# HGRN scores: two of seven levels copied on ScalarE, and the fourth sums of pairs split one block later

## Chip, core and metric

The kernel runs on one core of a Trainium2 chip. The core has TensorE (PE) for matrix products, VectorE (DVE) and ScalarE (ACT) for elementwise work, GpSimd (POOL), and SyncE (SP), which starts most transfers. TensorE writes into PSUM, in banks that the other engines must empty; everything else lies in SBUF. The engines run side by side and wait for one another through semaphores; each takes its own instructions strictly in order. The metric is the device time of one execution in microseconds (us); smaller is better.

## What is computed

One inference step of a hybrid encoder layer: an mLSTM branch and an HGRN2 branch on 512 prompt frames and 32 sample frames, merged by gates. The change touches the HGRN branch. Its core, per head (8 heads, 128 channels each), with a running state `S` (key x value):

```python
def _hgrn_chunk(S, inp):
    q, k, v, lf = inp
    causal = jnp.tril(jnp.ones((L, L), dtype=bool))[:, :, None]
    g = jnp.cumsum(lf, axis=2)
    dec = jnp.exp(jnp.where(causal, g[:, :, :, None, :] - g[:, :, None, :, :], -jnp.inf))
    a = jnp.einsum('bhtc,bhtsc,bhsc->bhts', q, dec, k)
    o = jnp.einsum('bhtc,bhce->bhte', q * jnp.exp(g), S) + jnp.einsum('bhts,bhse->bhte', a, v)
    ...
```

`a` are the scores: each pair (query frame t, key frame s) is decayed per channel by the product of the forget gates between s and t. The inputs `q`, `k`, `v`, `lf` and the gates are columns of one large projection `xn @ w_in`, in fp32.

## The kernel before

**Projections.** The large projection is cut into units of 128 columns. An fp32 operand is split into a high part (a cast on ScalarE, L130) and a low part (a subtraction on VectorE, L131), and one product takes three matmuls. Most units are computed two at a time by class `Two` (L387), with seven products in place of eight: weights `a11`, `a12`, `a22` as they are and four sums `s1` to `s4` of weight tiles. In the trace the split sums are called `ws1..` to `ws4..`, the plain ones `wa11..`, `wa12..`, `wa22..`, each followed by the unit's number and `h` or `l`. A product is a block of 12 matmuls, in two halves of 6.

The class keeps the sums in five buffers (`NSUM`). `begin` (L397) loads `s1` and `s3` with a transfer by SyncE (L402) and an accumulating transfer by GpSimd (L403). `form` (L442) splits a weight; when `s2` has been split, `s4` is made in the same buffer by another accumulating transfer on GpSimd (L460) for pairs that are `early`; the last pair of all is `alone` and adds on VectorE (L462). `split_piece` (L125) takes its tiles from a ring of five (`NPIECE`).

**The order of blocks.** Class `Pump` (L551) merges the blocks of successive pairs. For the HGRN pairs the times in `PAIR` give, from one pair to the next, the order `s2, s1, s3, a11', a12', a22, s4` (a prime marks the next pair). `steps` (L596) calls `prepare` (L580) ahead of each block, which makes ready the weights of all blocks up to `AHEAD = 3` further on. So `s4` is prepared ahead of the matmuls of the next pair's `a11'`, and the block behind it, the next pair's `s2` with its `s1`, is prepared one block later. The casts and subtractions of a block are put under `issue_after(self.behind)` (L592): they may not be issued on ScalarE before the instruction `behind`.

**The chain of a head.** `chain(h)` (L1483) is a generator. What it yields is the number of half blocks that the pump runs before the chain goes on, so that its matmuls lie between those of the projections. It computes the scores by seven levels, `LEVELS = (1, 2, 4, 8, 16, 32, 64)`: at level c it copies every other run of c keys into `km` on ScalarE (L1500), multiplies them on TensorE with the queries of the neighbouring runs (L1511), and multiplies keys and queries by one more stretch of gates on VectorE (L1535). Of the product of 128 x 256, the entries whose row and column numbers have an exclusive or of at least c belong to this level or a later one; they are written into `at` by a masked copy on VectorE (L1542), the later levels over the earlier. At level 16 the mask is 32 columns wider, for the sample. `at` is set to zero on GpSimd at the start (L1487); at the end the triangles are cut out on GpSimd (L1479), which also zeroes the diagonal. Before each level's `km` the chain sets `pump.behind` to the `km` before it (L1498). After the levels come transposes of values and keys (L1587, copied to SBUF in L1590), the update of the state (`su`, L1606), the outputs (`ho`, L1630), their norm (`osb`, L1651), and the finish of the head before (`hoT`, L1659 and L1660), which lies behind level 16 of the next chain.

**What sets the order.** TensorE's order is written out by hand (`manual_schedule`). On the other engines a planner orders the instructions ahead of time: by priority and by the times at which its own model of the machine has them ready. The priority is the order in which the program is written, unless `high_priority` raises it, as it does for `km`, for the scores' copies and for the copies out of PSUM.

Of the kernel before, what the change touches and what calls it, by code (L numbers as in the profile page):

```python
# [17 lines left out]
P = 128  # L18
# [26 lines left out]
LEAD = 3  # L45
NPIECE = 5
AHEAD = 3
SCRATCH = 1024
RAWAHEAD = 4
WQ = 256  # L50
# [14 lines left out]
def hybrid_step(ctx: ExitStack, tc: tile.TileContext, a, o):  # L65
    nc = tc.nc
    V, S, G, PE = nc.vector, nc.scalar, nc.gpsimd, nc.tensor
# [10 lines left out]
    def slot(name, dt=F32):  # L78
        return sp.tile([P, SLOT], dt, tag="s", name=name)
# [5 lines left out]
    def small(name, shape, dt=F32, bufs=2, tag=None):  # L85
        return tp.tile(shape, dt, tag=tag or name, name=name, bufs=bufs)
# [11 lines left out]
    def paux(name):  # L98
        return pa.tile([P, 2, 512], F32, tag="a", name=name)
# [18 lines left out]
    def raw_piece(src, name):  # L118
        raw = wp.tile([P, WP], F32, tag="wr", name=name, bufs=NRAW)
        nc.sync.dma_start(raw[:, : src.shape[-1]], src)  # L120
        return raw
# [208 lines left out]
    class One:  # L330
# [22 lines left out]
        def prepare(self, i):  # L353
            def make(raw):
                if i == 0:
                    self.w = []
                self.w.append(split_piece(raw[self.unit, i], f"wi{self.unit}{i}"))

            return make
# [27 lines left out]
    class Two:  # L387
# [45 lines left out]
        def make(self, *forms):  # L433
            def go(raw):
                with tc.high_priority() if self.apart else nullcontext():
                    for form in forms:
                        if form not in self.w:
                            self.form(form, raw)

            return go  # L440

        def form(self, form, raw):  # L442
# [108 lines left out]
    class Pump:  # L551
# [28 lines left out]
        def prepare(self, upto):  # L580
            while self.made < min(upto, self.limit or len(self.order)):
                b = self.order[self.made]
                while self.begins and self.begins[0][0] <= self.made:
                    self.begins.pop(0)[1].begin()
                if b[1]:
                    need = self.loads.index(b[1][-1]) + 1
                    for u, i in self.loads[self.loaded : need + RAWAHEAD]:
                        self.raw[u, i] = raw_piece(w_in[u][:, i * WP : (i + 1) * WP], f"wi{u}r{i}")
                    self.loaded = max(self.loaded, min(need + RAWAHEAD, len(self.loads)))
                if b[2]:  # L590
                    after = self.pairs if isinstance(self.todo[self.ids[self.made][0]], Two) and self.pairs else self.behind
                    with tc.issue_after(after.ins) if after is not None else nullcontext():  # L592
                        b[2](self.raw)
                self.made += 1

        def steps(self):  # L596
            for i, b in enumerate(self.order):
                self.prepare(i + 1 + AHEAD)
                yield from b[3]()
# [15 lines left out]
        def run(self, chain):  # L615
            for n in chain:
                self.to(self.done + n)
# [554 lines left out]
    def level_masks():  # L1172
        lmask, smask = masks()
        sxt = small("sxt", [P, P + 2 * NS], bufs=1, tag="vsm")
        nc.sync.dma_start(sxt, a["sxt"])
        for i, c in enumerate(LEVELS):
            V.tensor_scalar(
                lmask[:, i, : 2 * P].rearrange("p (b t) -> p b t", b=2),
                sxt[:, :P].rearrange("p (o t) -> p o t", o=1).to_broadcast([P, 2, P]),
                float(c),  # L1180
                None,
                ALU.is_ge,
            )
        V.tensor_scalar(smask, sxt[:, P : P + NS], 0.5, None, ALU.is_ge)
        V.tensor_scalar(lmask[:, QUADS, 2 * P :], sxt[:, P + NS :], 0.5, None, ALU.is_ge)
        return lmask, smask

    with tc.manual_schedule(engines={mybir.EngineType.Activation, mybir.EngineType.DVE, mybir.EngineType.PE}):
# [15 lines left out]
        for k in range(KD):  # L1204
            t = xt[k]
# [129 lines left out]
    with tc.manual_schedule(engines={mybir.EngineType.PE}):  # L1335
        for h in range(MH):
# [35 lines left out]
            if h == 0:  # L1372
                with tc.issue_after(last.ins):
                    lmask, smask = level_masks()
# [6 lines left out]
    NA = NP // 2  # L1381
# [4 lines left out]
    def view(t, off, dims):  # L1386
        base = t[:, 0:T]
        return bass.AP(base.tensor, base.offset + off, [list(base.ap[0])] + [list(d) for d in dims])
# [94 lines left out]
    def chain(h):  # L1483

        tf, kk, q0, qq, kq, ii = (hs[h][k] for k in ("tf", "kk", "q0", "qq", "kq", "ii"))
        at = tp.tile([P, NA + P], F32, tag="bc", name=f"at{h}")
        G.memset(at, 0.0)  # L1487
        snap = small("snap", [P, 2, QUADS, NS], bufs=1, tag="ksm")
        dg = small("dg", [P, 5])
        told = tf[:, :T]  # L1490
# [3 lines left out]
        for li, c in enumerate(LEVELS):  # L1494
            smp = li == QUADS
            n = HB if smp else NA
            km = tp.tile([P, NA], F32, tag="vs", name=f"km{h}{c}", bufs=1)
            pump.behind = held[-1] if held else None  # L1498
            with tc.high_priority():
                low = S.copy(  # L1500
                    km.rearrange("p (n j c) -> p n j c", j=2, c=c),
                    view(kk, HB, ((2 * c, NA // (2 * c)), (c - HB, 2), (1, c))),
                )
                if li < QUADS:
                    S.copy(snap[:, :, li], hs[h]["pair"][:, :, csmp])
            held.append(low)
            yield STEPS[li]

            pn = paux(f"pl{h}{c}")
            for b in range(2):  # L1510
                PE.matmul(  # L1511
                    pn[:, 0, b * P : (b + 1) * P],
                    km[:, b * P : (b + 1) * P],
                    view(qq, b * P, ((2 * c, P // (2 * c)), (HB + c, 2), (1, c))),
                    start=True,
                    stop=True,
                )
            if smp:
                PE.matmul(pn[:, 0, NA:HB], kk[:, NA : NA + P], qq[:, csmp], start=True, stop=True)  # L1519
                ks, qs = (snap[:, i].rearrange("p l t -> p (l t)") for i in range(2))  # L1520
                PE.matmul(pn[:, 1, :P], ks, qs, start=True, stop=True)
            nb, na = (HB if c < NS else NA) // (2 * c), NA // (2 * c)
            tb, ta = told[:, : 2 * nb], told[:, told.shape[-1] - 2 * na :]
            tn = ttmp[:, base : base + nb + na]
            sides = ((tb, 0, nb, 1, 0), (ta, HB, na, 0, nb))
            with tc.high_priority():
                for t, lo, m, first, _ in sides:

                    x = view(
                        kk, lo + first * c, ((qoff + (1 - 2 * first) * c, 2), (2 * c, m), (1, c))  # L1530
                    )
                    d = bass.AP(
                        t.tensor, t.offset + 1 - first, [list(t.ap[0]), [2 * first - 1, 2], [2, m], [0, c]]
                    )
                    V.tensor_tensor(x, x, d, ALU.mult)  # L1535
                if told.shape[-1] == 2 * (nb + na):
                    t = told.rearrange("p (n t) -> p n t", t=2)
                    V.tensor_tensor(tn, t[:, :, 0], t[:, :, 1], ALU.mult)
                else:
                    for t, _, m, _, o_ in sides:  # L1540
                        V.tensor_tensor(tn[:, o_ : o_ + m], t[:, ::2], t[:, 1::2], ALU.mult)
                V.copy_predicated(at[:, :n], lmask[:, li, :n], pn[:, 0, :n])  # L1542
                if smp:
                    for i in range(QUADS):
                        d = slice(i * NS, (i + 1) * NS)
                        V.copy_predicated(at[d, NA:HB], smask[d], pn[d, 1, d])
            base += nb + na
            if c == NS // 2:
                tsmp = tn[:, nb - 1 : nb]
            told = tn  # L1550
            if li == 0:

                yield 1
                pn = paux(f"pd{h}")
                for b, c_ in enumerate([c_ for c_, _, _ in chunks] + [slice(NA, NA + P)]):
                    PE.transpose(pn[:, b // NB, b % NB * P : (b % NB + 1) * P], kq[:, c_], ident)
                with tc.high_priority():
                    V.tensor_reduce(
                        dg, pn.rearrange("p a t -> p (a t)")[:, : 5 * P].rearrange("p (b t) -> p b t", t=P), AX.X, ALU.add
                    )  # L1560
            if li == 4 and h:
                yield 1
                finish(h - 1)
# [40 lines left out]
        for b in range(NB):  # L1604
            c = slice(b * P, (b + 1) * P)
# [22 lines left out]
        for b, (c, i, j) in enumerate(chunks):  # L1628
            d = slice(b * P, (b + 1) * P)
# [56 lines left out]
    for k in range(2):  # L1686
        t = slot(f"p{k}")
# [17 lines left out]
    for f in range(KD):  # L1705
        w = weight(a["w_brh"][f], f"wbh{f}")
        acc = dense(w, 0, P, P, obs, f"yb{f}")
        t = gbs[f]
# [8 lines left out]
    for f in range(KD):  # L1717
        t = slot(f"h1{f}")
# [167 lines left out]
```

## Time and profile before

| quantity | us |
|---|---|
| median of three runs | 1139.38 (1138.98 to 1142.49) |
| the profiled execution | 1136.01 |
| its span, first to last instruction | 1134.3 |
| HGRN stage (640 to 955), of the span | 315 |
| of that: the last chain and the blocks behind it (864 to 955) | 91 |

The profile shows one execution. For each engine it gives the busy time, and for an instruction its start, its duration, and in brackets the time that its engine stood idle before it with what ended that time. A line such as `L1542 DVE COPY_PREDICATED at<-lmask,pl` names the line of the program, the engine, the operation, and the tiles written and read. A number behind the unit's name is left out in groups. The matmuls overlap: one of 272 columns is drawn with 0.29 us, though the next starts well before its end, so the distance between starts tells more than the durations.

### The profile page before, as it was taken

The page shows a single profiled execution, that of the slowest core. Times are in us where ns is not written, and L with a number is a line of the kernel's source. Part 1 is how long each engine was busy: PE and PEld are TensorE (multiplying, and loading weights), DVE is VectorE, ACT ScalarE, POOL GpSimd, SP SyncE. Part 2 cuts the span into 40 slices and gives each one's busy share as a digit, 9 for nine tenths or more (in the row PEclk, how much of TensorE's full clock was granted, in tenths as well). Part 3 has the DMA queues.
Part 4 walks back from the last instruction along what each step waited for, and adds up shares of the span by engine and source line. Part 5 has one row for each costly group of instructions (what it writes and reads, how often), then busy time and mean ns, then how long its engine had stood idle before and what let it go on. Part 6 is the DMA issues. An engine that isn't in the chain of part 4 may idle for free.

```text
span 1134.3 us, 24068 instructions
## 1 busy us (share of the span) xinstructions
PE 1116.8 (98%) x8849; PEld 1101.4 (97%) x8849; DVE 896.5 (79%) x2027; ACT 680.2 (60%) x1537; POOL 185.9 (16%) x363
## 2 busy tenths in 40 slices
PE   9999999999999999999999999999999999999998
PEld 8999999999999999999999999999998999999998
DVE  6887998576896786976888699999999867654585
ACT  5677557655666555665665477677766657333462
POOL 4842010100010100101000122223232220000000
PEclk9999999999999999999999999999999999999999
DMA  7134224323344142552767766666666686332743
GB/s 236 56 96 133 79 75 159 118 95 106 132 152 151 49 131 105 158 168 69 239 163 234 180 145 143 138 140 140 148 149 165 174 222 172 113 103 70 269 141 116
DMA packets 91006, 159.68 MB, mean 141 GB/s; under 512 B 10245, under 2 KB 17797, under 8 KB 90889
## 3 DMA queue, kind: packets, MB, share of 16 engines
q1 hardware_dynamic: 80928, 140.27, 38.3%
q0 software_dynamic: 9792, 17.83, 10.1%
q8 instruction: 69, 1.13, 0.4%
q14 instruction: 49, 0.39, 0.1%
q10 hardware_dynamic: 168, 0.06, 0.0%
HBM read 133.21 MB, written 24.91 MB: 139 GB/s over the span
## 4 chain that ended last, share of the span: by engine, by line
PE 78%; DVE 10%; DMA 5%; ACT 3%; issue 2%; POOL 0%; SPq 0%; ACTq 0%; DVEq 0%
PE d L485 29%; PE ya L151 8%; PE pg L1736 4%; PE q L151 4%; PE yb L151 4%; PE o L151 4%; PE C L902 4%; PE k L151 4%; DMA ws<-in_w_in 3%; PE sc L862 3%; PE nm L1077 2%; PE pl L1511 2%; PE d L370 1%; DVE cv L634 1%; PE ple L151 1%
## 5 line engine op out<-in xcount | busy, mean ns | idle before, releaser
L403 POOL DMA_DIRECT2D ws<-in_w_in x46 | 40.3, 876 | 230.3 <-DVE rsq_u L168 30.3
L499 ACT COPY t<-d 128x272 f32<-128x272 f32 x126 | 47.7, 379 | 3.2 <-PE d L485 3.1
L1535 DVE TENSOR_TENSOR hkq<-hkq,q 128x288 f32<-128x288 f32 (+1 forms) x96 | 40.8, 432 | 3.9 <-PE pl L1519 1.0
L634 DVE SCALAR_TENSOR_TENSOR cv<-ub,vec,cv 128x547 f32<-128x547 f32 x48 | 40.4, 842 | 1.3 <-ACT cv L629 0.6
L1511 PE MATMUL pl<-hkq,km 128*128 128x128 f32 x224 | 38.0, 292 | 1.8 <-ACT km L1500 1.7
L1511 PEld LDWEIGHTS pl<-hkq,km 128*128 128x128 f32 x224 | 31.1, 189 | 3.9 <-ACT km L1500 3.4
L1500 ACT COPY km<-hkq 128x256 f32<-128x256 f32 x56 | 24.0, 428 | 15.6 <-DVE hkq L1535 6.2
L1006 DVE SCALAR_TENSOR_TENSOR c<-c,wi,Cs 128x258 f32<-128x258 f32 x32 | 15.3, 479 | 20.0 <-PE Cs L1004 19.8
L460 POOL DMA_DIRECT2D ws<-in_w_in x22 | 23.2, 1055 | 41.0 <-DVE ws272l L131 27.4
L914 ACT COPY Co<-C 128x258 f32<-128x258 f32 x32 | 10.4, 378 | 29.1 <-PE C L902 22.3
L1145 DVE TENSOR_TENSOR y<-ya,y 128x272 f32<-128x272 f32 x48 | 19.1, 436 | 10.3 <-PE ya L151 9.2
L1542 DVE COPY_PREDICATED at<-lmask,pl 128x256 f32<-128x256 uint8 (+1 forms) x56 | 25.3, 451 | 0.0
L1088 ACT COPY y<-nm 128x516 f32<-128x516 f32 x16 | 9.5, 591 | 21.6 <-PE nm L1077 21.5
L799 POOL COPY vsm<-vt 128x96 f32<-128x96 f32 x16 | 6.0, 382 | 88.2 <-ACT vt L510 44.7
L1479 POOL TENSOR_SCALAR_AFFINE_SELECT aa<-at 128x128 f32<-128x128 f32 x32 | 18.8, 621 | 8.9 <-DVE at L1542 8.9
L1077 PE MATMUL nm<-vhl,sh 128*128 128x258 f32 x112 | 18.3, 285 | 0.0
L1036 DVE BATCH_NORM_STATS2 bs<-y 128x6 f32<-128x512 f32 (+1 forms) x20 | 13.8, 688 | 5.5 <-ACT y L1088 5.5
L1723 DVE TENSOR_TENSOR h<-o,h 128x272 f32<-128x272 f32 x16 | 6.3, 436 | 14.5 <-PE o L151 14.5
L978 POOL CAST vhl<-one 128x4 fp32r<-128x4 f32 x8 | 2.0, 244 | 95.8 <-PE nm L1077 95.8
L876 ACT CAST sh<-dm 128x512 fp32r<-128x512 f32 (+3 forms) x16 | 7.3, 459 | 16.6 <-DVE dm L870 16.6
L1641 ACT ACTIVATE osq<-kq 128x128 f32<-128x128 f32 x32 | 9.8, 305 | 12.3 <-DVE kq L1636 12.1
L1710 DVE TENSOR_TENSOR gb<-yb,gb 128x272 f32<-128x272 f32 x16 | 6.3, 436 | 13.1 <-PE yb L151 13.1
(4490 smaller groups left out, 5072.9 us busy)
## 6 DMA issues: line engine op xcount, KB each, us to landing
ws<-in_w_in POOLq DMA_DIRECT2D x68, 256.0 KB, 4.8
ws<-in_w_in SPq DMA_DIRECT2D x46, 256.0 KB, 3.6
ya_d<-y SPq DMA_DIRECT2D x32, 272.0 KB, 2.7
y<-ya_d SPq DMA_DIRECT2D x24, 272.0 KB, 3.7
c<-in_C SPq DMA_DIRECT2D x16, 258.0 KB, 3.9
out_Cp<-Co SPq DMA_DIRECT2D x16, 258.0 KB, 2.5
out_Cs<-c SPq DMA_DIRECT2D x16, 258.0 KB, 2.8
x<-in_xT SPq DMA_DIRECT2D x8, 272.5 KB, 4.7
```

Source lines behind the costliest of these rows:

```text
L151: PE.matmul(both[b][:m, :TH], part(w, off + k * step, m, x), xx[:, half(b)], start=(k == 0 and j == 0), stop=(k == n - 1 and j == 2),)
L403: G.dma_start(t, w_in[u][:, i * WP : (i + 1) * WP], accum_op=ALU.add)
L485: PE.matmul(ps, ww[:, c], xx, start=(start and k == 0 and j == 0), stop=end, skip_group_check=not start,)
L499: S.copy(t, ps)
L634: V.scalar_tensor_tensor(cv[:, :547], ub[:, j : j + 547], vcol(V_CW + 4 * ft + j), cv[:, :547], ALU.mult, ALU.add)
L862: PE.matmul(pn[:, 0, :n], ks[f][x][:, j * P : (j + 1) * P], qs[f][y][:, NS + j * P : T], start=(f == 0 and i == 0), stop=(f == KH - 1 and ...
L902: PE.matmul(pn[g][:, :VH], kw[b][x][:, f * P : (f + 1) * P], vv[b][y][:, g * VH : (g + 1) * VH], start=(b == 0 and j == 0), stop=(b == NB ...
L1077: PE.matmul(pn[:, g, :VH], st[j][x][:, (i - j) * P : (i - j + 1) * P], vv[j][y][:, g * VH : (g + 1) * VH], start=(j == 0 and q == 0), stop ...
L1511: PE.matmul(pn[:, 0, b * P : (b + 1) * P], km[:, b * P : (b + 1) * P], view(qq, b * P, ((2 * c, P // (2 * c)), (HB + c, 2), (1, c))), star ...
L1535: V.tensor_tensor(x, x, d, ALU.mult)
L1542: V.copy_predicated(at[:, :n], lmask[:, li, :n], pn[:, 0, :n])
L1736: PE.matmul(ps, part(w, k * P, P, x), xx[:, c], start=(k == 0 and j == 0), stop=(k == KD - 1 and j == 2))
```

## The change

Two edits, in the HGRN stage and in the blocks woven into it.

The scores: at the first level (c = 1), where the mask leaves out only the diagonal, the product is copied whole into the first 256 columns of `at` by ScalarE. At the last level (c = 64), where the mask is two off-diagonal blocks of 64 x 64 in each half, ScalarE copies these blocks, with one instruction for each half of the partitions. The five levels between keep the masked copy on VectorE. GpSimd sets only the last 128 columns of `at` to zero.

The fourth sums: for every `early` pair but the last, the block `s4` is prepared one block later, together with the block behind it; nothing behind it is prepared earlier or later than before.

```diff
+LATE = 2
...
+            go.late = self.early and not self.alone and forms == ("s4",)
             return go
...
         def prepare(self, upto):
             while self.made < min(upto, self.limit or len(self.order)):
                 b = self.order[self.made]
+                if getattr(b[2], "late", False) and self.made > upto - LATE:
+                    break
...
         at = tp.tile([P, NA + P], F32, tag="bc", name=f"at{h}")
-        G.memset(at, 0.0)
+        G.memset(at[:, NA:], 0.0)
...
-                V.copy_predicated(at[:, :n], lmask[:, li, :n], pn[:, 0, :n])
+                if li == 0:
+                    S.copy(at[:, :NA], pn[:, 0, :NA])
+                elif c == P // 2:
+                    for d, e in ((slice(0, c), slice(c, P)), (slice(c, P), slice(0, c))):
+                        S.copy(
+                            at[d, :NA].rearrange("p (b t) -> p b t", b=2)[:, :, e],
+                            pn[d, 0, :NA].rearrange("p (b t) -> p b t", b=2)[:, :, e],
+                        )
+                else:
+                    V.copy_predicated(at[:, :n], lmask[:, li, :n], pn[:, 0, :n])
```

## The prediction, made before the result

> **What bounds the kernel now.** I read the page's busy times first, then the busy times of the stretch in which the changed functions run, then the waits of TensorE in that stretch, and last, for each wait, the timeline of the engine that is named in it.
>
> ```profile
> span 1134.3 us, 24068 instructions
> PE 1116.8 (98%) x8849; PEld 1101.4 (97%) x8849; DVE 896.5 (79%) x2027; ACT 680.2 (60%) x1537; POOL 185.9 (16%) x363
> ...
> 640.00:955.00 315.00, 310.11 (x2488) 306.36 (x2487) 281.47 (x737) 214.84 (x568) 81.89 (x115) 1.00 0.67 156
> 640.00:864.00 224.00, 223.14 (x1796) 220.29 (x1795) 213.23 (x586) 159.68 (x441) 64.50 (x92) 1.00 0.64 144
> 864.00:955.00 91.00, 86.96 (x694) 86.07 (x693) 68.24 (x152) 55.17 (x129) 17.38 (x23) 1.00 0.73 183
> ```
>
> TensorE bounds it. The eight HGRN heads and the pairs of projections woven into them fill 640 to 955 us. The columns after the length are PE, PEld, DVE, ACT, POOL. PE idles 315 - 310.11 = 4.9 us there, 4.0 of them after 864. Counted by weight loads the slack is 315 - 306.36 = 8.6 us. The clock is 1.00 throughout, so nothing is to be had from it. VectorE is nearly full as well (213.23 of 224, 95%), ScalarE is at 71%. So the change can only win what is left of 4.9 to 8.6 us, and whatever it costs must stay under a bound of the same kind. [...]
>
> PE's idle is in few places. Rows of the timeline, the bracket being the idle time before the instruction and what ended it:
>
> ```profile
> 664.43 0.71 PE L1511 MATMUL pl<-hkq,km 128*128 128x128 f32 x4 [0.30 <-ACT km L1500]
> 726.95 0.71 PE L1511 MATMUL pl<-hkq,km 128*128 128x128 f32 x4 [0.40 <-ACT km L1500]
> 869.19 0.74 PE L1511 MATMUL pl<-hkq,km 128*128 128x128 f32 x4 [0.73 <-ACT km L1500]
> 872.46 0.75 PE L1511 MATMUL pl<-hkq,km 128*128 128x128 f32 x4 [0.25 <-ACT km L1500]
> 878.99 0.33 PE L1660 MATMUL hoT<-anti,osb 128*128 128x128 f32 x1 [1.44 <-DVE osb L1651]
> 921.30 0.39 PE L485 MATMUL d<-xfh,ws384h 128*128 128x272 f32 x1 [1.62 <-ACT t L499]
> ```
>
> They add up to 4.74 us: four waits for a key copy `km`, one for the normalised output `osb` of the last head but one, one for a copy of a pair's partial product.
>
> **Why km and osb are late.** The last chain, then an earlier head, ScalarE and VectorE in order of time:
>
> ```profile
> 866.31 0.79 DVE L1535 TENSOR_TENSOR hkq<-hkq,q 128x288 f32<-128x288 f32 x2
> 868.21 0.62 ACT L130 CAST ws480h<-ws 128x512 fp32r<-128x512 f32 x1 [2.80 <-DMA ws<-in_w_in]
> 868.73 0.40 ACT L1500 COPY km<-hkq 128x256 f32<-128x256 f32 x1
> 868.86 0.69 DVE L131 TENSOR_TENSOR ws480l<-ws,ws480h 128x512 fp32r<-128x512 f32 x1 [1.36 <-ACT ws480h L130]
> ...
> 725.63 0.42 DVE L1535 TENSOR_TENSOR hkq<-hkq,q 128x256 f32<-128x256 f32 x1
> 725.98 0.62 ACT L130 CAST ws475h<-ws 128x512 fp32r<-128x512 f32 x1 [1.79 <-DMA ws<-in_w_in]
> 726.50 0.40 ACT L1500 COPY km<-hkq 128x256 f32<-128x256 f32 x1
> ```
>
> `ws4..h` is the cast of a pair's fourth sum. Its data come by an accumulating DMA that is not there yet, so ScalarE stands for 2.80 us with `km` queued behind it, although `km`'s input was ready at 867.1; VectorE stands for 1.36 us in turn. At 726 it is the same in small: `km` could have gone at 726.05 and went at 726.50.
>
> **Part 1, the late split of the fourth sums** (`go.late`, `LATE`). It removes nothing and adds no instruction: per pair, one cast (ACT) and one subtraction (DVE) are prepared one block of 12 matmuls later, directly ahead of the next pair's first sums. What keeps the order on ScalarE is `issue_after(self.behind)`: the cast may not be issued ahead of the `km` copy that was last when the block was prepared. For the pairs of queries, and for the pair of 868, the move crosses the matmuls of level 2, so that the cast now comes behind that level's `km` instead of ahead of it. The consumers have room:
>
> ```profile
> 793.15 0.68 DVE L131 TENSOR_TENSOR ws477l<-ws,ws477h 128x512 fp32r<-128x512 f32 x1
> 798.39 0.29 PE L485 MATMUL d<-xh,ws477l 128*128 128x272 f32 x1
> ```
>
> 798.39 - 793.83 = 4.6 us against one block of about 2 us. In the last chain `km` then goes at 867.1, PE does not stand at 869.19, and VectorE is kept from 1.36 us of standing, but not wholly: ws480's data land at 868.2 in any case, and only small steps can fill the time before. From there to `osb` VectorE works without a gap, so what PE gets back at 878.99 is what VectorE gets back: bounds 0 (a fresh stall takes its place) and 0.73 + 0.25 + 1.44 = 2.42; I take **-1.2**, most of 1.36, as the rest is bound by the DMA. At 664 and 726 I take the visible waits, 0.30 + 0.40: **-0.7**, bounds 0 and -0.7. Each of these four waits also costs a slower restart (0.39 at 921.30 for a matmul that takes 0.29 in a run): 4 x 0.1 = **-0.4**, bounds 0 and -0.4.
>
> **Part 2, the scores.** Per head two of seven masked copies leave VectorE; ScalarE gets one copy of 128 x 256 and two of 64 partitions x 128. The memset of `at` shrinks from 384 to 128 columns on GpSimd, which is busy 82 of 315 us: nothing. Prices by rows of the same stretch:
>
> ```profile
> L1542 DVE COPY_PREDICATED at<-lmask,pl 128x256 f32<-128x256 uint8 (+1 forms) x56 | 25.3, 451 | 0.0
> ...
> L499 ACT COPY t<-d 128x272 f32<-128x272 f32 x66 | 25.1, 380 | 3.2 <-PE d L485 3.1
> L1500 ACT COPY km<-hkq 128x256 f32<-128x256 f32 x55 | 23.5, 427 | 15.6 <-DVE hkq L1535 6.2 <-DVE hr L169 4.0 <-DVE rsq_u L168 3.0
> L1594 ACT COPY kit<-ht 128x128 f32<-128x128 f32 x8 | 2.2, 272 | 0.0
> ...
> 729.22 0.45 DVE L1542 COPY_PREDICATED at<-lmask,pl 128x256 f32<-128x256 uint8 x1
> 729.55 0.29 DVE L1538 TENSOR_TENSOR q<-q 128x136 f32<-128x136 f32 x1
> 729.76 0.69 DVE L131 TENSOR_TENSOR wa1252l<-wi52r,wa1252h 128x512 fp32r<-128x512 f32 x1
> ...
> 730.25 0.29 PE L485 MATMUL d<-xl,wa1252h 128*128 128x272 f32 x1
> 730.50 0.39 PE L485 MATMUL d<-xh,wa1252l 128*128 128x272 f32 x1
> ...
> 853.56 0.29 PE L485 MATMUL d<-xl,wa1280h 128*128 128x272 f32 x1
> 853.83 0.40 PE L485 MATMUL d<-xh,wa1280l 128*128 128x272 f32 x1
> ...
> 921.30 33.46 PE d L485 x264
> ```
>
> A masked copy lasts 0.45 us, but the next instruction starts 0.33 after it, so VectorE is relieved by 0.66 us a head. The copy of the last level stands right ahead of `wa1252l`, which ends at 730.45, and PE's first matmul with it follows at 730.50: 0.25 after its neighbour, where the spacing in an unbroken run is 33.46 / 264 = 0.127 (the last row, from the chain of waits). So PE waits some 0.13 here and restarts 0.1 slower, in six heads alike, the last at 853.83: 6 x 0.23 = **-1.4**, bounds 0 and -1.4. On level 0 no wait of PE hangs on VectorE; nothing. ScalarE pays 0.38 (by `t`, also out of PSUM) + 2 x 0.27 (by `kit`, the same width out of PSUM, its lower end; 0.43 each by `km` is the upper) = 0.92 us a head. It has the room: 315 - 214.84 = 100 us idle over eight heads; and the copy of level 0 lies in a time when `km` waits for VectorE anyway. I take **0**, with the case in which the place is wrong as the first rival. The copies' own waits are for matmuls whose results VectorE waited for before; GpSimd's triangles now wait for ScalarE, at a time when it is ready earlier than VectorE was.
>
> **The tail.** In the blocks after the last chain a later fourth sum may hold SyncE, whose queue waits for that sum's buffer:
>
> ```profile
> 911.34 0.69 DVE L131 TENSOR_TENSOR ws490l<-ws,ws490h 128x512 fp32r<-128x512 f32 x1 [1.96 <-ACT ws490h L130]
> ...
> 912.06 0.33 SPq L402 DMA_DIRECT2D ws<-in_w_in  x1
> ...
> 912.91 0.42 SPq L1689 DMA_DIRECT2D p<-in_pT  x1
> ...
> 917.24 0.65 ACT L103 CAST ps0h<-p 128x544 fp32r<-128x544 f32 x1 [2.48 <-DMA p<-in_pT]
> ```
>
> The transfer of `p` follows the release at 912.03 within a microsecond, and the wait at 921.30 comes from ScalarE's 2.48 for it. If the release moves by a block (1.5 us without a chain), that wait grows by up to 1.5; if it comes earlier, it shrinks by up to 1.62. The cast already stands directly ahead of the next pair's first sum there, so I take **0**.
>
> **Sum:** -1.2 - 0.7 - 0.4 - 1.4 = -3.7 us. The profiled execution took 1136.01 (span 1134.3 and 1.7 around it), so it would take 1132.3. The median of the runs shown is 3.4 above it; the same step from 1139.38 gives **1135.7**.
>
> **Rivals.**
>
> *A. ScalarE becomes the pacer ahead of the state update.* Between the last `km` of a head and the copy of the transposed keys it runs without a gap:
>
> ```profile
> 787.13 0.62 ACT L130 CAST ws477h<-ws 128x512 fp32r<-128x512 f32 x1 [0.95 <-PE d L485]
> 788.14 0.41 ACT L1500 COPY km<-hkq 128x256 f32<-128x256 f32 x1 [0.39 <-DVE hkq L1535]
> ...
> 792.29 0.58 ACT L1590 COPY hkq<-ht 128x512 f32<-128x512 f32 x1
> ...
> 793.50 1.05 PE L1606 MATMUL su<-hi,hkq 128*128 128x128 f32 x8
> ```
>
> The copy ends at 792.87, 0.63 ahead of `su`. If the fourth sum's cast moves into this stretch (0.52, from 868.21 to 868.73) and the two copies come with 0.27 to 0.41 each (`kit`, and the `km` of 788.14), it is 1.06 to 1.34 late. PE then waits 0.43 to 0.71 in each of eight heads, and what was won ahead of `su` is spent there: +3.4 to +5.7, from 1139.38 some 1144. It decides from a delay of 0.63 on. For it: no gap and little slack; against it: the scalings of the values in that stretch are not urgent and the key copy has high priority, so that it may pass them.
>
> *B. The late split moves nothing.* ws475h went at 725.98 although the program prepares it ahead of a block that PE starts at 728: casts are placed when they are ready, not where they are written. Then only the scores act: -1.4 and a few tenths where 0.33 of VectorE helps `osb`: 1137.7, no change.
>
> *C. All waits go,* that of 921.30 too: -4.74 - 1.4 - 0.5 of restarts = -6.6, 1132.8. For it speaks that upstream relief moves the release at 912.03; against it that the order on ScalarE there is untouched.
>
> **How the numbers follow.** About 0.3% (3.4 us) is what a measurement of this kernel can tell from no change; the forecast lies just beyond. Forecast 0.45, of which 0.35 beyond the bound; A 0.25, slower; B 0.17, of which 0.15 no change; C 0.13, faster. Faster 0.50, same 0.25, slower 0.25. The range takes in C with the cap of 8.6 us (1130.8) and A to its upper price (1145.1): 1131 to 1145. The forecast's own range is 1134 to 1138, since its terms can each fall to nothing.
>
> **What would show it.** Right: no wait of PE on `km` at level 2 of the last chain, the cast of ws480 behind that `km`, the wait on `osb` down from 1.44 to a few tenths, `wa12..l` no longer ending as PE reaches it, DVE busy down by about 7 us and ACT up by about 7. Wrong: waits of `su` on the key copy (A), the casts ws4 in their old places (B), or waits of PE on first and second sums `ws1`, `ws2`, which now queue behind the fourth; also a reordering elsewhere in the planner's order that these steps don't see.

## The result, and the profile after

The changed kernel is slower: 1153.1 us median of four runs (1150.3 to 1153.46), against 1140.18 (1138.98 to 1142.49) for the kernel before, also four runs. The ratio is 1.0108, 95% interval [1.009, 1.0127]. The profiled execution took 1153.29 us. The page of the changed kernel, busy times first, then the busy times of the HGRN stretch (columns after the length: PE, PEld, DVE, ACT, POOL, clock):

```profile
span 1151.6 us, 24068 instructions
PE 1120.1 (97%) x8849; PEld 1103.0 (96%) x8849; DVE 894.8 (78%) x2011; ACT 686.0 (60%) x1561; POOL 180.0 (16%) x363
...
640.00:955.00 315.00, 295.07 (x2349) 289.53 (x2348) 266.69 (x698) 209.04 (x568) 75.25 (x114) 1.00 0.63 149
```

The span grew by 1151.6 - 1134.3 = 17.3 us. PE's idle time between 640 and 955 rose from 4.9 to 315 - 295.07 = 19.9 us, by weight loads from 8.6 to 25.5, which is 16.8 of the 17.3. So the loss lies in the changed stretch, and the clock, still 1.00, has no part in it. The window is the same 315 us, but the stage now ends later, so the window holds less of it: VectorE and ScalarE are less busy in it, not more. What PE waits for between 640 and 975, from the view of waits (us in all, times, longest):

```profile
PE pl L1515 <- ACT km L1504: 6.0, 9, 1.8
PE d L487 <- ACT t L501: 3.1, 2, 2.2
PE d L487 <- DVE ws288l L132: 1.9, 1, 1.9
PE ht L1601 <- POOL snap L1586: 1.3, 2, 0.7
PE d L487 <- DVE ws278l L132: 1.3, 1, 1.3
...
```

(The lines of the program have moved: 131 is now 132, 1500 is 1504, 1511 is 1515, 1535 is 1539, 1542 is 1555.) No wait on `osb` or on `wa12` is left, as predicted. New is a wait of about 1.25 us on the low half of a pair's second sum, in six heads alike (`ws274l` to `ws279l`) and of 1.9 on `ws288l`; new also are more waits on `km` and on the GpSimd copy `snap`. One of the six, in the changed kernel: first VectorE's timeline, then ScalarE's, then PE's.

```profile
782.10 0.69 DVE L132 TENSOR_TENSOR ws453l<-ws,ws453h 128x512 fp32r<-128x512 f32 x1
...
784.17 0.68 DVE L132 TENSOR_TENSOR ws177l<-ws,ws177h 128x512 fp32r<-128x512 f32 x1
784.77 0.68 DVE L1658 TENSOR_TENSOR kq<-kq,hr 128x512 f32<-128x512 f32 x1
...
786.95 0.68 DVE L450 TENSOR_TENSOR ws<-ws,wi77r 128x512 f32<-128x512 f32 x1
...
790.68 0.69 DVE L132 TENSOR_TENSOR ws277l<-ws,ws277h 128x512 fp32r<-128x512 f32 x1
...
781.00 0.41 ACT L1504 COPY km<-hkq 128x256 f32<-128x256 f32 x1 [2.05 <-DVE hkq L1539]
...
781.46 0.61 ACT L131 CAST ws453h<-ws 128x512 fp32r<-128x512 f32 x1
...
796.03 0.62 ACT L131 CAST ws477h<-ws 128x512 fp32r<-128x512 f32 x1 [2.15 <-DMA ws<-in_w_in]
...
791.43 0.39 PE L487 MATMUL d<-xfh,ws277l 128*128 128x272 f32 x1 [1.25 <-DVE ws277l L132]
```

The same places in the kernel before, VectorE, ScalarE, PE:

```profile
774.76 0.69 DVE L131 TENSOR_TENSOR ws453l<-ws,ws453h 128x512 fp32r<-128x512 f32 x1
...
775.68 0.69 DVE L131 TENSOR_TENSOR ws177l<-ws,ws177h 128x512 fp32r<-128x512 f32 x1
...
777.75 0.69 DVE L448 TENSOR_TENSOR ws<-ws,wi77r 128x512 f32<-128x512 f32 x1
...
780.55 0.69 DVE L131 TENSOR_TENSOR ws277l<-ws,ws277h 128x512 fp32r<-128x512 f32 x1
...
773.44 0.62 ACT L130 CAST ws453h<-ws 128x512 fp32r<-128x512 f32 x1 [0.93 <-DMA ws<-in_w_in]
774.55 0.41 ACT L1500 COPY km<-hkq 128x256 f32<-128x256 f32 x1 [0.49 <-DVE hkq L1535]
...
783.88 0.29 PE L485 MATMUL d<-xfh,ws277l 128*128 128x272 f32 x1
```

Before, the cast of the fourth sum `ws453h` ran ahead of `km`, in time that ScalarE would have stood anyway; now it runs behind `km`, and ScalarE stands 2.05 us ahead of it. On VectorE the fourth sum's low half and the next pair's first sum were 0.92 us apart, now 2.07, with the work of level 4 between them; from the fourth sum's low half to the second sum's it took 5.79 us before and 8.58 now. So `ws277l`, which ended at 781.24 and had 2.6 us to spare, ends at 791.37, while PE wanted it at 790.18. The next fourth sum is accumulated into the buffer of the second after that, so the lag comes back one pair later: the cast `ws477h` waits 2.15 us for its transfer.

A measure by head makes kernels comparable: the time from VectorE's first multiplication of the second chain to that of the eighth, six steady heads. The two rows of it, before and after:

```profile
676.84 0.46 DVE L1535 TENSOR_TENSOR hkq<-hkq,tf 128x288 f32<-128x288 f32 x1 [0.22 <-PE pl L1511]
...
862.21 0.46 DVE L1535 TENSOR_TENSOR hkq<-hkq,tf 128x288 f32<-128x288 f32 x1 [0.23 <-PE pl L1511]
```

```profile
677.76 0.46 DVE L1539 TENSOR_TENSOR hkq<-hkq,tf 128x288 f32<-128x288 f32 x1 [0.22 <-PE pl L1515]
...
874.20 0.47 DVE L1539 TENSOR_TENSOR hkq<-hkq,tf 128x288 f32<-128x288 f32 x1 [0.22 <-PE pl L1515]
```

That is 185.4 us before and 196.4 after: 11.1 of the 17.3 us arise in six heads, 1.85 in each. The six waits on second sums are 7.5 of it, and the waits on `km` there grew from 0.4 to 2.7. "Six heads" below is this figure.

### The profile page after: what moved, and what is told of

Read it like the earlier page. It is cut to its first block, busy times and chain, and to the rows that moved or that the text cites. A ratio compares the mean times of both kernels' runs of the same rounds, so it can differ in the third digit from the quotient of the medians.

```text
span 1151.6 us, 24068 instructions
## 1 busy us (share of the span) xinstructions
PE 1120.1 (97%) x8849; PEld 1103.0 (96%) x8849; DVE 894.8 (78%) x2011; ACT 686.0 (60%) x1561; POOL 180.0 (16%) x363
## 4 chain that ended last, share of the span: by engine, by line
PE 80%; DVE 9%; DMA 4%; ACT 3%; issue 2%; POOL 1%; SPq 0%; ACTq 0%; DVEq 0%; POOLq 0%
PE d L487 31%; PE ya L152 8%; PE pg L1749 4%; PE q L152 4%; PE yb L152 4%; PE o L152 4%; PE C L906 4%; PE k L152 4%; DMA ws<-in_w_in 3%; PE sc L866 3%; PE pl L1515 2%; PE nm L1081 2%; PE d L371 1%; DVE cv L638 1%; PE ple L152 1%
## 5 line engine op out<-in xcount | busy, mean ns | idle before, releaser
L1010 DVE SCALAR_TENSOR_TENSOR c<-c,wi,Cs 128x258 f32<-128x258 f32 x32 | 15.3, 478 | 20.0 <-PE Cs L1008 19.9
L1555 DVE COPY_PREDICATED at<-lmask,pl 128x256 f32<-128x256 uint8 (+1 forms) x40 | 18.0, 450 | 0.0
L880 ACT CAST sh<-dm 128x512 fp32r<-128x512 f32 (+3 forms) x16 | 7.4, 460 | 16.8 <-DVE dm L874 16.8
L816 ACT ACTIVATE kf<-k 128x272 f32<-128x272 f32 x32 | 10.9, 391 | 9.4 <-PE k L152 6.8
```

## The experiments

| run | six heads, us | median, us | ratio to before, 95% interval |
|---|---|---|---|
| before (profile above) | 185.4 | | |
| the change (profile above) | 196.4 | 1153.1 | 1.0108 [1.009, 1.0127] |
| e1 late split alone | 203.4 | 1154.4 | 1.0137 [1.0118, 1.0156] |
| e2 scores alone | 187.1 | 1140.03 | 1.0005 [0.9988, 1.0023] |
| e3 first level alone | 188.2 | 1140.75 | 1.0012 [0.9995, 1.003] |
| e4 last level alone | 186.5 | 1139.11 | 0.9989 [0.9973, 1.0005] |
| e5 late, queries only | 206.3 | 1154.64 | 1.0127 [1.0109, 1.0144] |
| e6 late, from unit 80 on | 185.7 | 1139.11 | 0.9996 [0.9984, 1.0008] |
| e7 late, `wa11` raised | 203.1 | 1154.7 | 1.0137 [1.0116, 1.0157] |
| e8 change, sums raised | 190.4 | 1144.47 | 1.0045 [1.0031, 1.0059] |
| e9 late, `wa11` and `ob` raised | 182.6 | 1133.43 | 0.9951 [0.9932, 0.9969] |
| e10 casts of `p` later | 185.6 | 1140.78 | 1.0015 [1.0002, 1.0028] |
| e11 scores alone, once more | 186.8 | 1137.87 | one run |
| e12 scores, casts of `p` later | 186.6 | 1141.64 | 1.0024 [1.0012, 1.0037] |
| e13 `wa11` and `ob` raised only | 184.1 | 1135.4 | 0.9973 [0.9958, 0.9988] |
| e14 late, `ob` raised | 186.6 | 1138.44 | 0.9995 [0.9982, 1.0007] |
| e15 scores, both raised | 186.2 | 1140.91 | 1.001 [0.9993, 1.0027] |
| e16 change, both raised | 207.4 | 1164.65 | 1.0221 [1.02, 1.0242] |
| e17 as e9 | 182.8 | 1133.62 | 0.9946 [0.9928, 0.9964] |
| e18 as e13 | 185.1 | 1136.55 | 0.9975 [0.9965, 0.9985] |

Each ratio is to runs of the kernel before on the same chip.

### Which of the two edits (e1 to e4)

e1 is the changed kernel with the scores of before; e2 is the changed kernel without the late split; e3 and e4 have one level's copy each, without the late split. The edit of e2:

```diff
-LATE = 2
+LATE = 1
```

> Only the late split; the scores as before. Theory Q (the late fourth sum queues ahead of the next pair's first and second sums, and the second sums reach TensorE too late): about the whole loss is here, 1149 to 1155, with waits of PE on ws2..l of about 1.2 us in six heads. Theory S (the copies on ScalarE shift the planner's order, and the late split is harmless): 1137 to 1141, no such waits.

> Only the copies on ScalarE; the fourth sums prepared as before. Theory Q: 1136 to 1140, wa12..l no longer just in time, no waits of PE on ws2..l. Theory S: 1149 to 1155, with those waits.

> Only the first level's copy on ScalarE, the rest as before. Theory Q: 1138 to 1141, no change. Theory S, if it is this copy that shifts the order: 1145 to 1155.

> Only the last level's copies on ScalarE, the rest as before. Theory Q: 1136 to 1140, the wait at wa12..l gone (0.23 us in six heads, -1.4). Theory S, if it is these copies that shift the order: 1145 to 1155.

The late split alone makes the whole loss, as theory Q has it, and a little more than the two edits together (in e1 the mean granted clock from 671 to 857 is 0.97, in the changed kernel 1.00; see the last section); the scores' intervals hold 1, and theory S falls. The waits are not where Q put them, though. PE waits in e1 for another tile than in the changed kernel: not for the second sum, but for the low half of the next pair's first plain weight, `wa11`. VectorE and PE of e1, and VectorE of the kernel before at the same place:

```profile
799.93 0.43 DVE L1555 COPY_PREDICATED at<-lmask,pl 128x256 f32<-128x256 uint8 x1
...
800.41 0.68 DVE L132 TENSOR_TENSOR wa1154l<-wi54r,wa1154h 128x512 fp32r<-128x512 f32 x1
...
801.14 0.40 PE L487 MATMUL d<-xh,wa1154l 128*128 128x272 f32 x1 [1.82 <-DVE wa1154l L132]
```

```profile
788.61 0.69 DVE L131 TENSOR_TENSOR wa1154l<-wi54r,wa1154h 128x512 fp32r<-128x512 f32 x1
...
790.87 0.44 DVE L1542 COPY_PREDICATED at<-lmask,pl 128x256 f32<-128x256 uint8 x1
```

In the kernel before `wa1154l` stands ahead of the masked copy of the last level, in e1 behind it. Its cast was long done in both cases; only VectorE's turn is late. So the late sum pushes something of the next pair behind the chain's work on VectorE, and it isn't always the same tile.

### Place or bound, and which pairs (e5, e6)

The late split does two things: it moves the place in the program where the fourth sum is prepared, and with it the instruction `behind` that binds its cast. A kernel with the late place and the `behind` of before has, on every engine, the same instructions in the same order as the kernel before: the place does nothing, the bound does all. For the pairs of gates and values the late split moves no instruction either; only the pairs of queries (units 49 to 55) and the first pair of merge gates (unit 80) cross a `km`.

```diff
-            go.late = self.early and not self.alone and forms == ("s4",)
+            go.late = self.early and not self.alone and forms == ("s4",) and 45 <= self.unit < 57
```

(e6: `and self.unit >= 80`; both with the scores of before.)

> Old scores; the fourth sum is split one block later only in the seven pairs of queries and forget gates (units 49 to 55). Of the pairs of gates and values no instruction changes its place in either form, so if the loss is made in the steady heads, this is all of it: 1152 to 1156 us against 1139.7 of the kernel before, six waits of PE of about 1.8 us on the low halves of wa1151 to wa1155 and wa1180. If instead the blocks behind the last chain make it (pairs of unit 80 on), the time is that of before, 1138 to 1141.

> Old scores; the fourth sum is split one block later only in the pairs of merge gates (unit 80 on), so in the last chain alone: one cast and one subtraction go behind the level-2 key copy of that chain. The prediction's term for the last chain, by itself: -1.2 us with 0.2 of restarts, so 1138.3 against 1139.7, the waits of 0.73 on that km and of 1.44 on osb smaller. If the relief is spent by another stall behind it, 1139.5 to 1141 and the sum of PE's waits from 864 to 955 unchanged at 4.0.

The seven pairs of queries are the whole loss: e5 has the six waits on `wa11` that were expected. The last chain's own late split wins nothing. PE's waits of e6 from 860 to 960:

```profile
PE hoT L1673 <- DVE osb L1664: 1.4, 1, 1.4
PE pl L1515 <- ACT km L1504: 1.0, 1, 1.0
```

The wait on the `km` behind `ws480h` is gone, as predicted (it is called level 2 there, counted from 0: that of runs of 4 keys), and the one at the level behind it, 0.25 before, is now 1.0; `osb` is as late as before. A fresh stall took its place, the lower bound that the prediction gave for this term.

### Place on VectorE or VectorE's order (e7, e8)

Theory V says that only VectorE's order makes the loss; theory P says that the fourth sum in its new place costs the time, whatever stands last. e7 raises the priority of `wa11` in e1, e8 that of the first and second sums in the changed kernel.

```diff
-                with tc.high_priority() if self.apart else nullcontext():
+                with tc.high_priority() if self.apart or self.early and forms == ("a11",) else nullcontext():
```

(e8: `or self.early and "s2" in forms`.)

> Late split of all fourth sums with the old scores, as in the run that took 1154.4, and the cast and subtraction of the next pair's first plain weight (wa11) put at high priority, so that VectorE takes the low half ahead of the masked copies of levels 32 and 64 instead of behind them. Theory V (the loss is VectorE's order: the later fourth sum pushes one low half of the next pair behind the chain's work): the six waits of 1.8 us go, time 1140 to 1144. Theory P (the fourth sum's cast and subtraction in their new place cost the time themselves, whatever stands last): the waits turn up on other tiles, km or the first and second sums, time 1151 to 1155.

> The changed kernel, with the split of the first and second sums and the addition between them put at high priority, so that they do not fall behind the work of levels 8 and 16 on VectorE. Theory V: the six waits of 1.25 us on the low half of the second sums go, with 1.9 on ws288 and the late accumulating transfers of the fourth sums behind them, time 1139 to 1143 against 1153.1 without it. Theory P: 1149 to 1154, the waits on other tiles.

e8 went the way of V, though not all of it: the six waits on the second sums are gone and 8.6 of the 13 us with them; what is left are eight waits of up to 0.9 us on `km`, and its time, 1144.47, lies between the ranges of the two theories. e7 went the way of P: the waits on `wa11` are gone and six of 2.1 to 2.5 us stand elsewhere. The view of waits of e7, and its VectorE there:

```profile
PE ht L1600 <- DVE at L1555: 13.1, 6, 2.5
```

```profile
798.77 0.43 DVE L1555 COPY_PREDICATED at<-lmask,pl 128x256 f32<-128x256 uint8 x1
...
799.31 0.25 DVE L1677 SCALAR_TENSOR_TENSOR ob<-hoT,vec,hg 128x32 f32<-128x32 f32 x1
```

The transposes `ht` wait for a PSUM buffer. There are two of this kind; one is held by the scores of the last level until their masked copy, the other by `hoT` of the head before until the small product `ob` (L1677). Before, that product ran at 786.18, before level 32; in e7 it stands behind the last level. So it was again a VectorE instruction that had slipped, one that frees a buffer.

### Restoring VectorE's order (e9, e14, e13, e17, e18)

e9 raises the two products `ob` too; e14 raises them alone; e13 is e9 without the late split. All have the scores of before.

```diff
-        V.scalar_tensor_tensor(ob[:, NS:T], pt[:, 0, :], g, gg[:, NS:T], ALU.mult, ALU.mult)
-        V.scalar_tensor_tensor(ob[:, :NS], pt[:, 1, P - NS : P], g, gg[:, :NS], ALU.mult, ALU.mult)
+        with tc.high_priority():
+            V.scalar_tensor_tensor(ob[:, NS:T], pt[:, 0, :], g, gg[:, NS:T], ALU.mult, ALU.mult)
+            V.scalar_tensor_tensor(ob[:, :NS], pt[:, 1, P - NS : P], g, gg[:, :NS], ALU.mult, ALU.mult)
```

> Late split of all fourth sums with the old scores, the cast and subtraction of the next pair's first plain weight at high priority (as in the run that took 1154.7), and now also the two products `ob` of the head before, whose PSUM buffer the next transposes otherwise do without. VectorE then does the same work as before in almost the order of before. Theory V (only VectorE's order made the loss): no wait of PE over 1 us in the heads, the transposes no longer wait for the last level's copy (2.1 us, six times), time 1139 to 1143. Theory P (the fourth sum's new place costs the time whatever stands last): another wait of about 2 us a head, time 1150 to 1155.

> The kernel before (old scores, old split), with the same two groups of VectorE's work at high priority as in the run that took 1133.43 (the first plain weight of the next pair, and the products `ob` of the head before). If that run's gain comes from the raised work alone: 1132 to 1135. If the late split itself wins what the prediction gave it in the heads and the last chain (2.3 us) once VectorE's order no longer spoils it: 1135 to 1138, that is 2 to 3 us behind it.

> Late split of all fourth sums, old scores, and only the products `ob` of the head before at high priority; the first plain weight keeps its low priority, yet in the planner's order it now stands ahead of the last level's masked copy again, where it stands in the kernel before. Theory V: no wait of 1.8 us on wa11, time 1134 to 1142. If the raise of wa11 is what cured the run of 1133.43: the six waits are back, 1150 to 1155.

e14 decides between V and P: the late split is as late as in e1, the two products are raised, nothing else is edited, and the loss of 1.4% is gone (0.9995). ScalarE, VectorE and PE of e14:

```profile
775.18 0.41 ACT L1504 COPY km<-hkq 128x256 f32<-128x256 f32 x1 [2.02 <-DVE hkq L1539]
...
775.63 0.62 ACT L131 CAST ws453h<-ws 128x512 fp32r<-128x512 f32 x1
...
784.21 0.91 DVE L1676 SCALAR_TENSOR_TENSOR ob<-hoT,vec,hg 128x512 f32<-128x512 f32 x2
...
789.57 0.69 DVE L132 TENSOR_TENSOR wa1154l<-wi54r,wa1154h 128x512 fp32r<-128x512 f32 x1
...
791.73 0.43 DVE L1555 COPY_PREDICATED at<-lmask,pl 128x256 f32<-128x256 uint8 x1
...
790.31 0.40 PE L487 MATMUL d<-xh,wa1154l 128*128 128x272 f32 x1
```

The cast of the fourth sum stands behind `km` as in e1, and ScalarE stands 2.02 us there (2.04 in e1); but `wa1154l` is again ahead of the last masked copy, and PE takes it without a wait. Left are waits of 0.2 to 0.5 us on `wa12` in the six heads, 1.9 in all. What the raise of `ob` is worth by itself, with the old split, was not run. With both raised, e9 is faster than the kernel before (0.9951 [0.9932, 0.9969]) and below the ranges of both theories, and no wait of PE is on record in its six heads. To see what is the split's own part, e9 and e13 ran once more side by side:

> The run that took 1133.43 beside the one that took 1135.40, both on one chip and in five rounds, to settle what the late split is worth by itself once VectorE's order is mended. By the prediction's terms for the heads and the last chain (2.3 us) this one is 2.3 us below the other, 1133 to 1134. If the gain is the raised work's alone, the two are within 0.7 us.

> The same two raised groups with the old split, beside the kernel with the late split: 1135 to 1136 and 2.3 us above it if the late split wins what was predicted, the same within 0.7 us if it wins nothing.

1133.62 against 1136.55 on one chip: the late split is worth 1136.55 - 1133.62 = 2.9 us there; the intervals [0.9928, 0.9964] and [0.9965, 0.9985] do not overlap. In the six heads it is 182.8 against 185.1, in the first pair of runs 182.6 against 184.1. The prediction had 2.3 for Part 1.

### The same raise on the changed kernel (e15, e16)

> Both edits of the scores with the old split, and the two groups of VectorE's work at high priority. If the relief of VectorE by the scores (0.66 us a head) is worth something once the order is mended: 1131 to 1133. If the heads stay bound by TensorE there: 1133 to 1136, the same as the raise alone.

> The changed kernel with the two groups at high priority. In the planner's order the low half of the second sum still stands behind the work of level 16, where PE waited 1.25 us for it in six heads. Theory V: these waits stay or grow, since the raised work goes ahead of it too, time 1148 to 1158. If instead raising any of it frees the head as a whole: 1133 to 1140.

With the scores on ScalarE the planner puts the second sum of e16 behind the raised work too, and the wait on it grows from 1.25 to 2.1 in six heads:

```profile
PE d L487 <- DVE ws277l L132: 2.1, 1, 2.1
```

That is theory V once more, from the other side: the raise that takes 21 us off e1 (1154.4 to 1133.43) adds 11.5 to the changed kernel (1153.1 to 1164.65). Its size was missed (1148 to 1158 expected), and the clock has a part in it: cut into ten stretches of 31 to 40 us from 640 to 960, e16's profile has a mean granted clock of 0.89 (671 to 702) to 1.00, the changed kernel's 1.00. What e16's stretches lack of 1.00, times their lengths, adds up to some 10 us, an estimate. e15 is 5.5 us behind e13 and outside both of its ranges: with the raise, the scores cost time.

### The tail (e10 to e12)

PE waits in most profiles for a copy of a partial product behind the cast of `p`: 1.62 us in the profile of before, up to 4.1 in others. e10 binds the casts of `p` behind later sigmoids of the gates, e12 does the same with the new scores; e11 is e2 once more.

```diff
-            ps_.append(split(t[:, :T], f"ps{k}"))
+        with tc.issue_after(sigs[-1 if k else -3].ins):
+            ps_.append(split(t[:, :T], f"ps{k}"))
```

(`sigs` holds the sigmoids in `merge_a`.)

> The kernel before, with the casts of `p` on ScalarE put behind the sigmoids of the merge gates, so that ScalarE does not stand for the transfer of `p` with the copies of partial products queued behind it. It tells whether PE's wait at 921 (1.62 us in the profile of before, 4.0 in two later profiles, each of these with the clock at half for about 3 us behind it) hides what the edits do. If it does: that wait is gone, clock 1.00 throughout, 1133 to 1136 against 1139.7. If the next transfer takes its place: 1138 to 1140.

> Both edits of the scores without the late split once more, one look beside the two runs with the later casts of `p`: 1136 to 1143, as the run of 1140.03, and the same wait of PE on the copy behind `p` (1.6 or 4.0 us) that decides where it lies in that range.

> Both edits of the scores, no late split, and the casts of `p` behind the sigmoids. If the prediction's -1.4 us for the scores is real and was only hidden behind the varying wait for `p`: 1.4 below the kernel with the later casts alone. If the heads lose at level 8 what the low halves wa12 and osb gain: the same as that kernel within 0.5 us.

A miss: in e10 the same wait, 3.9 us, stands a block later, and the time is no better. e12 is no faster than e10, so the scores' 1.4 us was not hidden behind this wait.

## Why the prediction was wrong

**What bounds.** TensorE bounds, and only the 4.9 to 8.6 us of its idle time was to be won: this held, the best kernel here (e17) is 1139.85 - 1133.62 = 6.2 us below before. That VectorE was at 95% in the steady heads was quoted too, and its meaning was missed: with 213.23 of 224 us filled, what comes first on VectorE decided here what was late.

**Part 1, the step that failed:** "It removes nothing and adds no instruction" and "The consumers have room". Both are true of the fourth sum: `ws477l` still ended 5 us ahead of its use. But the step looked at this one consumer. The bound on one cast, seven times, let the planner arrange VectorE's work of the whole head anew, and there a low half of the *next* pair, or a product that frees a PSUM buffer, came to stand behind the chain's work. Predicted were -1.2 - 0.7 - 0.4 = -2.3 us; measured alone, e1, +14.7 (1154.4 - 1139.66). In e1's six heads, 18.0 us longer than before, the six waits on `wa11` are 11.0 us; the granted clock, 0.97 in the mean from 671 to 857, makes by estimate 0.03 x 186 = 5.6 us more in that stretch.

The wait that Part 1 was to remove was there to be won, and was buried under the order: from e18 to e17 the six heads get 2.3 us shorter, and the distances between the starts of PE's matmuls put it at those that take `km`, of levels 8 and 64 (8.8 us against 6.4, summed over the six heads). That the whole, 2.9, comes so near the predicted 2.3 is in part luck, since the places differ: 1.2 and a share of the restarts were put into the last chain, whose term came out at its bound of 0 in e6, and where the waits on `km` are 1.5 us in e17 and 0.8 in e18; the heads were given only the visible 0.7 and the other restarts.

**Part 2, the scores.** The gain came as predicted, and the price, put at 0, was larger: the low halves `wa12` are no longer just in time. In e2 VectorE ends one at 792.57, and PE takes it at 793.03:

```profile
791.89 0.68 DVE L132 TENSOR_TENSOR wa1254l<-wi54r,wa1254h 128x512 fp32r<-128x512 f32 x1
...
793.03 0.29 PE L487 MATMUL d<-xh,wa1254l 128*128 128x272 f32 x1
```

Yet the term of -1.4 measured 1.0005 [0.9988, 1.0023], and the six heads took 187.1, 186.8 and 186.6 us in three profiles with both scores against 185.4: 1.2 to 1.7 us longer. No wait of PE in e2 above 0.3 us names the cause, but the distances between the starts of its matmuls, added up from the traces, do. Over the six heads, compared with before, those at `wa12` are 1.4 us shorter, just the term; those at the matmuls that take `km` are 2.5 us longer, 1.0 of it at level 8 and 1.5 at level 16; and those of the products `su` are 0.55 longer. At level 16 ScalarE's order has changed: the activation `kq` of another unit now stands ahead of `km`, and ScalarE stands 0.69 us for its input, while in the kernel before `km` went first. ScalarE and PE of e2, and of the kernel before:

```profile
781.51 0.40 ACT L512 ACTIVATE kq<-d 128x272 f32<-128x272 f32 x1 [0.69 <-PE d L487]
781.80 0.40 ACT L1504 COPY km<-hkq 128x256 f32<-128x256 f32 x1
...
782.25 0.72 PE L1515 MATMUL pl<-hkq,km 128*128 128x128 f32 x4
```

```profile
780.67 0.41 ACT L1500 COPY km<-hkq 128x256 f32<-128x256 f32 x1 [0.64 <-DVE hr L169]
...
781.44 0.61 PE L1511 MATMUL pl<-hkq,km 128*128 128x128 f32 x4
```

So the step that failed in Part 2 is the "I take **0**" for ScalarE: its new copies fit into its idle time, but the order of the rest did not stay. Why `km` is late at level 8 stays open. Nor did the sign hold that VectorE's busy time falls by about 7 us: it fell from 896.5 to 894.8; why not by more, no run shows. One more price that was put at nothing shows: "GpSimd's triangles now wait for ScalarE, at a time when it is ready earlier". Being ready earlier, they went ahead of the copy `snap` in the last chain, on GpSimd of e2:

```profile
884.81 1.67 POOL L1483 TENSOR_SCALAR_AFFINE_SELECT aa<-at 128x128 f32<-128x128 f32 x4 [1.77 <-ACT at L1550]
886.44 0.74 POOL L1586 COPY snap<-hkq 128x128 f32<-128x128 f32 x1
...
887.23 0.33 PE L1601 MATMUL ht<-ident,snap 128*128 128x128 f32 x1 [0.81 <-POOL snap L1586]
```

PE waits 0.81 us for it, which it did not before.

**The tail** was put at 0. PE's waits for copies of partial products are 3.1 us after against 1.6 before; in the other profiles of this study they lie between 2.0 and 4.1, so this term can't be read from one of them.

**The rivals.** A, ScalarE as the pacer ahead of `su`: the sign was right, the place was not; no wait on `su` is among those of the changed kernel. Its mechanism shows in small in e2: the copy of the transposed keys ends at 794.24, 0.06 us ahead of `su`, where 0.63 was left before, and `su` takes the 0.55 us longer that were counted above. B, the split moves nothing: true for the pairs of gates and values, not for the queries. C, all waits go: no. The last sentence of the prediction, first and second sums queued behind the fourth and a reordering elsewhere in the planner's order, names what happened; it had been given no price and no chance.

What stays open: why the planner chose these places. Its own model of the times is in no profile.

## What to carry to other kernels

Where a planner orders the engines and one of them is 95% full, a new bound on one instruction can change the order of everything that engine does; its price here was not the moved instruction's time but that of whichever operand ended last. Read, for the full engine, how long ahead of their use the operands of the next stage end (`ws277l` had 2.6 us to spare and came 1.2 us late), and whether one of its instructions frees a PSUM buffer, before such a bound is costed at nothing. When a good local change loses, restore the order by priority before giving it up: here two short products turned +1.4% into no change, and two groups into a gain.

## What was not expected of the hardware

In e1 the clock granted to TensorE was 0.50 behind one wait of under 2 us, and 1.00 behind another. Two pairs of neighbouring stretches of 3.41 us (the first column after the length is PE's busy time, the sixth the granted clock):

```profile
764.52:767.93 3.41, 1.74 (x13) 1.29 (x12) 3.19 (x11) 3.36 (x10) 1.49 (x3) 1.00 0.50 73
767.93:771.34 3.41, 3.02 (x24) 3.02 (x25) 3.41 (x10) 1.80 (x6) 2.31 (x4) 1.00 0.30 94
...
798.65:802.06 3.41, 1.59 (x13) 1.37 (x12) 3.41 (x12) 2.67 (x8) 1.91 (x4) 1.00 0.58 77
802.06:805.47 3.41, 3.41 (x17) 3.41 (x17) 2.92 (x8) 1.70 (x5) 1.01 (x2) 0.50 0.51 151
```

In the stretch from 798.65 PE is idle for 3.41 - 1.59 = 1.82 us, the wait that ended at 801.14. In the next one the clock is 0.50, which by estimate costs 0.50 x 3.41 = 1.7 us, nearly the wait once more. The wait that ended at 768.32 is longer, 1.88 us; PE is idle for 3.41 - 1.74 = 1.67 us of the stretch from 764.52, the wait runs on into the next, and the clock is 1.00 in both. So the length of the wait did not tell in these two places whether the clock fell; what did, the rows do not show.

In e2 PE waited 4.08 us, until 924.00, for the copy of a partial product. In the four stretches of 2 us from 922 on the clock was 0.55, 0.50, 0.50 and 0.74, and matmuls of 272 columns started 0.23 us apart (924.39 to 925.53), against 0.127 in the unbroken run of the kernel before. What is missing from 1.00 makes by estimate 6.8 us at 0.50, more than the "about 3 us" that e10 expected of such a wait.

The mean granted clock of the whole profiled execution, all its waits included, is 0.991 in e1, 0.990 in e5 and 0.991 in e16. It is 1.0 in the kernel before and in the changed kernel, whose longest waits of PE from 640 to 975 are 1.62 and 2.2 us.
